# A two-layer hybrid encoder on one core: gate logits turned by full tiles, a projection's first products reordered, and the attention gating moved behind other casts

## The chip, the cores and the metric

The kernel runs on one core of one Trainium2 chip. The core has five engines with queues of their own: TensorE (PE, matrix products; its weight loads are shown apart as PEld), VectorE (DVE), ScalarE (ACT), GpSimd (POOL) and SyncE (SP, which here issues most transfers). The metric is the device time in microseconds of one execution; lower is better. Three runs of the kernel before give a median of 742.87 us.

## The reference

A bidirectional encoder trunk of two layers (`DEPTH = 2`) over 256 tokens and 1024 channels. In each layer the normalised input goes through one wide projection, whose parts feed two branches: a chunked gated DeltaNet that runs over the sequence in both directions, and a differential softmax attention with a partial rotation of q and k. Each branch is normalised and gated by SiLU, projected, weighed by a sigmoid gate and added; one output projection closes the layer.

```python
for l in range(DEPTH):
    h = rmsnorm(x, norm_w[l])
    proj = h @ w_in[l]
    (q_a, k_a, v_a, ab_a, z_a, q_b, k_b, v_b, z_b,
     gate_a, gate_b) = jnp.split(proj, SPLIT_IDX, axis=-1)
    y_a = gated_delta_branch(q_a, k_a, v_a, ab_a, z_a, conv_w[l], a_log[l], dt_bias[l], gdn_norm_w[l])
    lambda_init = 0.8 - 0.6 * math.exp(-0.3 * l)
    y_b = diff_attention_branch(q_b, k_b, v_b, z_b, cos, sin, diff_lambda[l], diff_subln_w[l], lambda_init)
    merged = (jax.nn.sigmoid(gate_a) * (y_a @ w_pa[l])
              + jax.nn.sigmoid(gate_b) * (y_b @ w_pb[l]))
    x = x + merged @ w_out[l]
return rmsnorm(x, final_norm_w)
```

Three places matter here. `ab_a` holds 32 gate logits per token: the rates beta and the decays of 8 heads in two directions. `q_b` is rotated before the attention. The end of the attention branch is

```python
    o = rmsnorm(o, subln_w) * (1.0 - lambda_init)
    o = o.transpose(0, 2, 1, 3).reshape(bsz, seq, DIFF_WIDTH)
    return o * jax.nn.silu(z)
```

## The kernel before

**Products in two halves.** Activations and weights are float32. Each is split into an upper half, the value cast to a shorter form (`hi`), and a lower half, the rest (`lo`), and a product is taken as three: upper by upper (line 324), upper by lower weights (325), lower activations by upper weights (326). A projection of 512 columns (`proj_tm`) goes over eight row blocks of the weights (`kt`) and, in each, over two tiles of 128 tokens (`m`). Its weights come in four pairs of row blocks (`kp`): `weights` loads a pair by a transfer on SP into `raw` (three buffers), casts it on ACT into `hi` (two buffers, line 308) and subtracts on DVE into `lo` (two buffers, line 310). `proj_fm` (385 to 389) does the same with the roles turned, for what the convolutions take.

**What sets the order.** The functions are written as a program, and a scheduler orders each engine's queue when the kernel is built: by priority, which is the order of the text unless a block is marked as of high priority, and by when operands are ready in its own timeline. `behind(x)` orders an instruction behind `x` on the same engine without a wait. On the chip each engine then takes its queue strictly in that order, and a wait stops all that stands behind it. `mark` collects instructions to be named later: `mark[nm, kp]` is the pair (cast on ACT, subtraction on DVE) of the weights of projection `nm`.

**Gate logits.** The 32 columns are projected with both halves of the weights beside each other, so that the sum lies in 64 rows of `abp` (line 630): rows 0 to 31 from the upper half, 32 to 63 from the lower. ACT copies them into `abT` (633), and one fp32 product per token tile with `id2`, two 32x32 identities one above the other, transposes and adds them at once (636). DVE copies the result into `ab` (638).

**The first rotated q.** `qk_part(s_, i)` projects half of q (`s_` = 0) or of k. The first, (0, 0), is written right behind the first half of the convolution's q, while ACT and DVE still evacuate that convolution and ACT takes logarithms and exponentials of the decays (lines 742 and 743). Behind it stand the small fp32 products `kk` of the keys with themselves (787), which have no fixed place.

**Gating the attention.** The attention's output `ob` (two halves `i` of the channels, two token tiles `m`, so four units) is multiplied by the norm's factor `rb` and by the gate `zb` (line 1197, four products on DVE), transposed in 32x32 blocks by DVE (line 249, `send`), written to DRAM on POOL's queue (251) and read back by four transfers on the same queue (257, `fetch`), which completes the transposition. `split_B` then makes its halves: the upper on ACT (263), the lower on DVE (265). All this runs beside the projections of the gates gb and ga, and beside the triangular merges (`join`) and the chunk steps (`chunks`) of the DeltaNet branch, which are of high priority. In that stretch TensorE takes, between the products of gb and ga, the merges y64p, zt, y128p and zt (lines 928, 943, 961), then y1p, sp, ks, y2p, qs and po (992 to 1031). The merges read `T64`, whose blocks DVE transposes at line 954. The sums of the keys' squares (`key_sums`, 1042 to 1054) use the same POOL queue behind the gating.

The places of the four units are given by marks: the gating of unit (0, m) behind the subtraction of pair 2 + m of gb's second half, that of (1, m) behind pair 1 + m of ga's first half; the splits of (0, m) behind pair 2 + m of ga's first half, of (1, m) behind pair 2 + m of its second half.

Of the kernel before, what the change touches and what calls it, by code (L numbers as in the profile page):

```python
# [8 lines left out]
F32 = mybir.dt.float32  # L9
# [3 lines left out]
ALU = mybir.AluOpType  # L13
# [4 lines left out]
P = 128  # L18
DM = 1024
KT = DM // P  # L20
SEQ = 256
NM = SEQ // P
# [27 lines left out]
def hybrid_encoder(  # L50
# [25 lines left out]
    const = pool("const")  # L76
# [18 lines left out]
    def bank_c(name):  # L95
        return ps_c.tile([P, 512], F32, tag="c", name=name)
# [4 lines left out]
    def last(ap, n):  # L101
# [7 lines left out]
    G.memset(ident, 1.0)  # L109
    G.affine_select(out=ident, in_=ident, compare_op=ALU.is_equal, fill=0.0,  # L110
                    base=0, pattern=[[1, P]], channel_multiplier=-1)
    id2 = const.tile([64, 32], F32, name="id2")
    V.tensor_tensor(id2, ident[0:64, 0:32], ident[0:64, 32:64], ALU.add)
    G.memset(tri, 1.0)
    for d, sg in ((0, 1), (1, -1)):
        G.affine_select(out=tri[:, d, :], in_=tri[:, d, :], compare_op=ALU.is_ge,
# [137 lines left out]
    def fetch(tb, dd, after):  # L254
        for j in range(4):
            with behind(after):
                G.dma_start(out=tb[blk(j)], in_=dd[:, :, j].rearrange("i t x -> t i x"))
# [55 lines left out]
                yield 2 * kp + k, hi[:, k, :n], lo[:, k, :n]  # L313

    def proj_tm(act, w, c0, n, evac, nm, places=(None,) * 4, spare=(), later=None, turned=(), between=None,
                banks=None, held=None, first=(), raws={}):

        accs = (banks or banks2)(f"pp_{nm}")
        for kt, hi, lo in weights(w, c0, n, nm, places, later=later, spare=spare, turned=turned, held=held,
                                  first=first, raws=raws):  # L320
            for m in range(NM):
                ts_ = slice(m * P, (m + 1) * P)
                o = accs[m][:, :n]
                T.matmul(o, act[kt // 4][:, 0, kt % 4, ts_], hi, start=kt == 0, stop=False)  # L324
                T.matmul(o, act[kt // 4][:, 0, kt % 4, ts_], lo, start=False, stop=False)  # L325
                mark["proj"] = T.matmul(o, act[kt // 4][:, 1, kt % 4, ts_], hi, start=False,  # L326
                                        stop=kt == KT - 1).ins
                mark["done", nm, kt] = mark["proj"]
        if between:
            between()  # L330
        for m in range(NM):
            evac(m, accs[m][:, :n])
# [174 lines left out]
    for l in range(DEPTH):  # L507
# [86 lines left out]
        def qk_part(s_, i):  # L594
                def evac_qk(m, ps):
                    st = work.tile([P, 512], F32, tag="w2a", name=f"stg{l}{s_}{i}{m}", bufs=2)
                    S.copy(st, ps)
                    g_ = st.rearrange("p (g e) -> p g e", e=DH)
                    x12 = g_[:, :, 0 : 2 * RD].rearrange("p g (x r) -> p g x r", x=2)
                    both = lambda t_: mid(mid(t_[:, m, :], 2), 8)  # L600
                    r4 = small.tile([P, 2, 8, 2, RD], F32, tag="r4", name=f"r4{l}{s_}{i}{m}", bufs=1)
                    V.tensor_tensor(r4[:, 0], x12, both(cos), ALU.mult)
                    V.tensor_tensor(r4[:, 1], x12, both(sin), ALU.mult)
                    V.tensor_tensor(x12[:, :, 0], r4[:, 0, :, 0], r4[:, 1, :, 1], ALU.subtract)
                    V.tensor_tensor(x12[:, :, 1], r4[:, 0, :, 1], r4[:, 1, :, 0], ALU.add)
                    pt = bank(f"qkt{l}{m}{s_}{i}")
                    for b in range(4):
                        T.transpose(pt[:, b * P : (b + 1) * P], st[:, b * P : (b + 1) * P], ident)

                    mark["qkT", m] = S.mul(qkT[i][:, s_, :, m * P : (m + 1) * P],  # L610
                                           pt.rearrange("p (b t) -> p b t", b=4), (DH ** -0.5, 1.0)[s_]).ins
                proj_tm(hT, wl, (C_QB, C_KB)[s_] + 512 * i, 512, evac_qk, f"qk{l}{s_}{i}",
                        turned=(0, 1) if (s_, i) == (0, 1) else ())

# [11 lines left out]
        for kt in range(KT):  # L628
            for part in range(2):
                T.matmul(abp[0:64, :SEQ], wabr[:, kt, :], hT[kt // 4][:, part, kt % 4, :],  # L630
                         start=kt == 0 and part == 0, stop=kt == KT - 1 and part == 1)
        abT = work.tile([64, SEQ], F32, tag="w2c", name=f"abT{l}", bufs=3)
        mark["ab"] = S.copy(abT, abp[0:64, :SEQ]).ins
        abq = bank_c(f"abq{l}")
        for m in range(NM):
            T.matmul(abq[:, m * 32 : (m + 1) * 32], abT[:, m * P : (m + 1) * P], id2,
                     start=True, stop=True)
        V.tensor_copy(ab.rearrange("p m c -> p (m c)"), abq[:, :64])

        a_ = small.tile([P, NM, 32], F32, tag="ga_", name=f"ga_{l}")  # L640
        V.tensor_scalar(a_[:, :, 0:16], ab[:, :, 0:16], -1.0, None, ALU.mult)
# [603 lines left out]
        V.scalar_tensor_tensor(rb, rb, 0.5 * (1.0 - lam0), r0, ALU.mult, ALU.mult)  # L1245

        ybT, yb_sent = pair(f"ybT{l}"), {}
        def gate_yb(i):
            at = [mark[f"ga{l}0", 1 + m][1] if i else mark[f"gb{l}1", 2 + m][1] for m in range(NM)]
            gated(lambda i, m: heads4(ob[i][:, m, :]), zb, rb, nw[:, 1:2], ybT, f"yb{l}",  # L1250
                  after={(i, m): at[m] for m in range(NM)}, halves_=(i,), sent=yb_sent)
            for m in range(NM):
                fetch(*yb_sent[i, m], None)

        gate_yb(0)
        gta = gate(C_GA, f"ga{l}", "eo", (lambda: gate_yb(1), None))
        for i, m in ((0, 0), (0, 1), (1, 0), (1, 1)):
            split_B(ybT[i], yb_sent[i, m][0], m, nw[:, 1:2], mark[f"ga{l}{i}", 2 + m])
        branch(ybT, w_pb[l], gtb, f"pb{l}")
# [137 lines left out]
```

## Time and profile before

| | |
|---|---|
| runs, median (lowest to highest) | 742.87 us (742.01 to 742.99), 3 runs |
| the profiled execution's own time | 742.73 us |
| its span, first to last instruction | 740.8 us |
| mean granted clock of TensorE | 0.997 |
| share of the span, DVE / ACT / POOL | 79% / 65% / 19% |
| transfers | 135.43 MB, mean 183 GB/s |

The page has the busy time of each engine, the span in 40 slices, the transfer queues, the chain of work that ended last, and the costliest groups of instructions. A row of the order of time reads: start in us, duration in us, engine, line, operation, the tile written, the tiles read, their shape, and a count where equal instructions are merged; a bracket gives the engine's idle time before it and what ended it. The ends of matmuls are modelled, so where the time of a matmul matters it is read from the starts of neighbours. A row of the waits reads: engine, tile and line that waited, what it waited for, then the total in us, how often, and the longest.

### The profile page before, as it was taken

The page shows a single profiled execution, that of the slowest core. Times are in us where ns is not written, and L with a number is a line of the kernel's source. Part 1 is how long each engine was busy: PE and PEld are TensorE (multiplying, and loading weights), DVE is VectorE, ACT ScalarE, POOL GpSimd, SP SyncE. Part 2 cuts the span into 40 slices and gives each one's busy share as a digit, 9 for nine tenths or more (in the row PEclk, how much of TensorE's full clock was granted, in tenths as well). Part 3 has the DMA queues.
Part 4 walks back from the last instruction along what each step waited for, and adds up shares of the span by engine and source line. Part 5 has one row for each costly group of instructions (what it writes and reads, how often), then busy time and mean ns, then how long its engine had stood idle before and what let it go on. Part 6 is the DMA issues. An engine that isn't in the chain of part 4 may idle for free.

```text
span 740.8 us, 13649 instructions
## 1 busy us (share of the span) xinstructions
PE 732.1 (99%) x5034; PEld 635.6 (86%) x5034; DVE 588.5 (79%) x1119; ACT 479.5 (65%) x1018; POOL 140.9 (19%) x223
## 2 busy tenths in 40 slices
PE   9999999999999999999999999999999999999996
PEld 6999889987888899888889899889788888998885
DVE  8696898999986885578667769999999769728782
ACT  6666875667876586645456578555787748665552
POOL 6004110112022433100000150202110514311000
PEclk9999999999999999999999999999999999999998
DMA  8755667776766473567674466767766736436641
GB/s 264 239 173 171 172 181 195 209 207 203 208 181 163 136 208 104 173 205 246 201 234 138 129 192 184 212 175 236 200 173 197 203 116 196 150 124 204 213 142 57
DMA packets 73732, 135.43 MB, mean 183 GB/s; under 512 B 12912, under 2 KB 13921, under 8 KB 73666
## 3 DMA queue, kind: packets, MB, share of 16 engines
q1 hardware_dynamic: 64750, 113.65, 51.6%
q0 software_dynamic: 7936, 19.35, 9.1%
q10 hardware_dynamic: 980, 1.58, 0.6%
q8 instruction: 39, 0.64, 0.4%
q14 instruction: 27, 0.22, 0.1%
HBM read 125.53 MB, written 9.01 MB: 182 GB/s over the span
## 4 chain that ended last, share of the span: by engine, by line
PE 96%; ACT 2%; issue 1%; DVE 1%; POOLq 0%; POOL 0%; DVEq 0%; ACTq 0%
PE pp_vb L369 4%; PE pp_qk L325 4%; PE pp_qk L326 3%; PE pp_qk L324 3%; PE sc L1067 2%; PE pp_o L369 2%; PE pp_za L325 2%; PE pf_k L385 2%; PE pf_v L385 2%; PE pf_v L389 2%; PE pp_ga L324 2%; PE pp_gb L324 2%; PE pp_zb L324 2%; PE pf_q L387 2%; PE pf_k L389 2%; PE pf_k L387 2%
## 5 line engine op out<-in xcount | busy, mean ns | idle before, releaser
L325 PE MATMUL pp_qk<-lo_qk,hT 128*128 128x512 f32 x128 | 50.5, 394 | 0.3
L326 PE MATMUL pp_qk<-hi_qk,hT 128*128 128x512 f32 x128 | 49.9, 390 | 0.0
L310 DVE TENSOR_TENSOR lo_qk<-raw_qk,hi_qk 128x1024 fp32r<-128x1024 f32 x32 | 39.1, 1221 | 12.0 <-ACT hi_qk L308 11.7
L324 PE MATMUL pp_qk<-hi_qk,hT 128*128 128x512 f32 x128 | 45.1, 393 | 0.0
L308 ACT CAST hi_qk<-raw_qk 128x1024 fp32r<-128x1024 f32 x28 | 29.4, 1049 | 23.4 <-PE pp_qk L326 12.7
L1077 ACT ACTIVATE es<-sc,mx 128x256 f32<-128x256 f32 x64 | 29.6, 473 | 19.5 <-DVE mx L1075 19.5
L385 PE MATMUL pf_q<-hT,hi_q 128*128 128x256 f32 x128 | 36.1, 285 | 0.0
L387 PE MATMUL pf_q<-hT,hi_q 128*128 128x256 f32 x128 | 35.9, 284 | 0.0
L385 PE MATMUL pf_k<-hT,hi_k 128*128 128x256 f32 x128 | 35.9, 286 | 0.0
L387 PE MATMUL pf_k<-hT,hi_k 128*128 128x256 f32 x128 | 35.9, 285 | 0.0
L385 PE MATMUL pf_v<-hT,hi_v 128*128 128x256 f32 x128 | 35.8, 285 | 0.0
L387 PE MATMUL pf_v<-hT,hi_v 128*128 128x256 f32 x128 | 35.8, 284 | 0.0
L389 PE MATMUL pf_q<-hT,lo_q 128*128 128x256 f32 x128 | 35.2, 288 | 0.0
L310 DVE TENSOR_TENSOR lo_pb<-raw_pb,hi_pb 128x1024 fp32r<-128x1024 f32 x16 | 19.6, 1225 | 18.9 <-ACT hi_pb L308 18.9
L389 PE MATMUL pf_v<-hT,lo_v 128*128 128x256 f32 x128 | 34.6, 288 | 0.0
L389 PE MATMUL pf_k<-hT,lo_k 128*128 128x256 f32 x128 | 34.3, 284 | 0.0
L308 ACT CAST hi_pa<-raw_pa 128x1024 fp32r<-128x1024 f32 x16 | 16.9, 1055 | 22.2 <-PE pp_pa L326 16.1
L679 DVE SCALAR_TENSOR_TENSOR cvq<-pf_q,cw,cvq 128x254 f32<-128x254 f32 (+1 forms) x64 | 30.0, 479 | 0.9 <-ACT cvq L675 0.4
L679 DVE SCALAR_TENSOR_TENSOR cvv<-pf_v,cw,cvv 128x254 f32<-128x254 f32 (+1 forms) x64 | 29.9, 479 | 0.1
L325 PEld LDWEIGHTS pp_qk<-lo_qk,hT 128*128 128x128 f32 x128 | 24.0, 188 | 6.6 <-DVE lo_qk L310 1.6
L679 DVE SCALAR_TENSOR_TENSOR cvk<-pf_k,cw,cvk 128x254 f32<-128x254 f32 (+1 forms) x64 | 28.5, 476 | 1.5 <-ACT cvk L675 0.9
L310 DVE TENSOR_TENSOR lo_pa<-raw_pa,hi_pa 128x1024 fp32r<-128x1024 f32 x16 | 19.6, 1224 | 11.2 <-ACT hi_pa L308 11.2
(416 smaller groups left out, 2535.1 us busy)
## 6 DMA issues: line engine op xcount, KB each, us to landing
raw_qk<-in_w_in_dram SPq DMA_DIRECT2D x32, 512.0 KB, 3.8
raw_k<-in_w_in_dram SPq DMA_DIRECT2D x16, 512.0 KB, 4.6
raw_q<-in_w_in_dram SPq DMA_DIRECT2D x16, 512.0 KB, 3.7
raw_v<-in_w_in_dram SPq DMA_DIRECT2D x16, 512.0 KB, 3.8
raw_zb<-in_w_in_dram SPq DMA_DIRECT2D x16, 512.0 KB, 4.0
raw_za<-in_w_in_dram SPq DMA_DIRECT2D x16, 512.0 KB, 3.8
raw_ga<-in_w_in_dram SPq DMA_DIRECT2D x16, 512.0 KB, 4.6
raw_pb<-in_w_pb_dram SPq DMA_DIRECT2D x16, 512.0 KB, 4.0
```

Source lines behind the costliest of these rows:

```text
L308: high = (V.tensor_copy if kp in turned else S.copy)(hi[:, :, :n], raw[:, :, :n]).ins
L310: mark[nm, kp] = high, V.tensor_tensor(lo[:, :, :n], raw[:, :, :n], hi[:, :, :n].bitcast(F32), ALU.subtract).ins
L324: T.matmul(o, act[kt // 4][:, 0, kt % 4, ts_], hi, start=kt == 0, stop=False)
L325: T.matmul(o, act[kt // 4][:, 0, kt % 4, ts_], lo, start=False, stop=False)
L326: mark["proj"] = T.matmul(o, act[kt // 4][:, 1, kt % 4, ts_], hi, start=False, stop=kt == KT - 1).ins
L369: mark["proj"] = T.matmul(o, act[kt // 4][:, pa, kt % 4, ts_], ws[kt][1 + pw], start=kt == 0 and n_ == 0, stop=kt == KT - 1 and n_ == 2).ins
L385: T.matmul(o, hi[:, cs], act[kt // 4][:, 0, kt % 4, :], start=first, stop=False, skip_group_check=True)
L387: T.matmul(o, hi[:, cs], act[kt // 4][:, 1, kt % 4, :], start=False, stop=False, skip_group_check=True)
L389: T.matmul(o, lo[:, cs], act[kt // 4][:, 0, kt % 4, :], start=False, stop=done, skip_group_check=True)
L679: V.scalar_tensor_tensor(ca[:, o0:o1], acc[:, b, o0 + sft : o1 + sft], cw[:, j, cb : cb + 1], ca[:, o0:o1], ALU.mult, ALU.add)
L1067: mm = T.matmul(sp[n][:, qt * SEQ : (qt + 1) * SEQ], qkT[h // 4][rows, 0, h % 4, qt * P : (qt + 1) * P], qkT[h // 4][rows, 1, h % 4, :], s ...
L1077: S.activation(es[:, n, qt, :], spv[:, qt, :], AF.Exp, bias=mx[:, n, qt : qt + 1], accum_out=s_all[:, h, n, qt : qt + 1])
```

## The change

Three edits.

1. The fold matrix `id2` and the addition that made it go. `abT` becomes a tile of 128 rows whose upper 64 rows POOL sets to zero; each token tile of it is transposed whole by the 128x128 identity, and DVE copies columns 0 to 31 and adds columns 32 to 63.
2. `proj_tm` gets a number `upper`. For the first `upper` row blocks it takes all products with the upper weights (both token tiles, both halves of the activations), and then those with the lower weights. It is 2 for the first half of the rotated q and 0 elsewhere. The same products are summed, in another order.
3. `gate_yb` does one unit at a time, with its reads right behind its write. Unit (0, 0) stays behind pair 2 of gb's second half; the other three follow pairs 0, 1 and 2 of ga's first half, in the order (0, 1), (1, 0), (1, 1), and are written behind the whole of that projection's products. For (1, 0) and (1, 1) these are the marks they had; (0, 1) had pair 3 of gb's second half. The splits keep their marks.

```diff
-    id2 = const.tile([64, 32], F32, name="id2")
-    V.tensor_tensor(id2, ident[0:64, 0:32], ident[0:64, 32:64], ALU.add)
...
     def proj_tm(act, w, c0, n, evac, nm, places=(None,) * 4, spare=(), later=None, turned=(), between=None,
-                banks=None, held=None, first=(), raws={}):
+                banks=None, held=None, first=(), raws={}, upper=0):
 
         accs = (banks or banks2)(f"pp_{nm}")
-        for kt, hi, lo in weights(w, c0, n, nm, places, later=later, spare=spare, turned=turned, held=held,
-                                  first=first, raws=raws):
+        parts = weights(w, c0, n, nm, places, later=later, spare=spare, turned=turned, held=held,
+                        first=first, raws=raws)
+        ws = [next(parts) for _ in range(upper)]
+        for part in range(2 if ws else 0):
+            for kt, hi, lo in ws:
+                for m in range(NM):
+                    for pa in range(2 - part):
+                        mark["proj"] = mark["done", nm, kt] = T.matmul(
+                            accs[m][:, :n], act[kt // 4][:, pa, kt % 4, m * P : (m + 1) * P], lo if part else hi,
+                            start=not (kt or pa or part), stop=False).ins
+        for kt, hi, lo in parts:
             for m in range(NM):
...
-                        turned=(0, 1) if (s_, i) == (0, 1) else ())
+                        turned=(0, 1) if (s_, i) == (0, 1) else (), upper=2 if (s_, i) == (0, 0) else 0)
...
-        abT = work.tile([64, SEQ], F32, tag="w2c", name=f"abT{l}", bufs=3)
-        mark["ab"] = S.copy(abT, abp[0:64, :SEQ]).ins
-        abq = bank_c(f"abq{l}")
+        abT = work.tile([P, SEQ], F32, tag="w2c", name=f"abT{l}", bufs=3)
+        G.memset(abT[64:P], 0.0)
+        mark["ab"] = S.copy(abT[0:64], abp[0:64, :SEQ]).ins
+        abq = bank_c(f"abq{l}")[:, :SEQ].rearrange("p (m c) -> p m c", m=NM)
         for m in range(NM):
-            T.matmul(abq[:, m * 32 : (m + 1) * 32], abT[:, m * P : (m + 1) * P], id2,
-                     start=True, stop=True)
-        V.tensor_copy(ab.rearrange("p m c -> p (m c)"), abq[:, :64])
+            T.transpose(abq[:, m, :], abT[:, m * P : (m + 1) * P], ident)
+        V.tensor_copy(ab, abq[:, :, 0:32])
+        V.tensor_tensor(ab, ab, abq[:, :, 32:64], ALU.add)
...
-        def gate_yb(i):
-            at = [mark[f"ga{l}0", 1 + m][1] if i else mark[f"gb{l}1", 2 + m][1] for m in range(NM)]
+        def gate_yb(i, m, at):
             gated(lambda i, m: heads4(ob[i][:, m, :]), zb, rb, nw[:, 1:2], ybT, f"yb{l}",
-                  after={(i, m): at[m] for m in range(NM)}, halves_=(i,), sent=yb_sent)
-            for m in range(NM):
-                fetch(*yb_sent[i, m], None)
-
-        gate_yb(0)
-        gta = gate(C_GA, f"ga{l}", "eo", (lambda: gate_yb(1), None))
+                  (m,), {(i, m): at}, (i,), yb_sent)
+            fetch(*yb_sent[i, m], None)
+
+        def gate_others():
+            for kp, (i, m) in enumerate(((0, 1), (1, 0), (1, 1))):
+                gate_yb(i, m, mark[f"ga{l}0", kp][1])
+
+        gate_yb(0, 0, mark[f"gb{l}1", 2][1])
+        gta = gate(C_GA, f"ga{l}", "eo", (gate_others, None))
```

## The prediction

> **What bounds the kernel now.** I read the page first, then who waited for whom, then the order of time around each edited place.
>
> ```profile
> span 740.8 us, 13649 instructions
> PE 732.1 (99%) x5034; PEld 635.6 (86%) x5034; DVE 588.5 (79%) x1119; ACT 479.5 (65%) x1018; POOL 140.9 (19%) x223
> PE 96%; ACT 2%; issue 1%; DVE 1%; POOLq 0%; POOL 0%; DVEq 0%; ACTq 0%
> ```
>
> TensorE is busy for 99% of the span and the chain of work that ended last is 96% TensorE. So an edit is worth something only where it shortens TensorE's own row of matmuls or one of the few holes in it. Work that DVE, ACT or POOL gains or loses counts only if TensorE then waits. Among the waits these two rows bear on the change:
>
> ```profile
> PEld pp_qk L325 <- DVE lo_qk L310: 1.6, 4, 0.6
> ACT ybT L263 <- DMA zb<-bny_yb: 2.6, 2, 1.6
> ```
>
> The first is a hole in TensorE's row (four waits for a lower weight half, 1.6 us in all, the longest 0.6). The second is ACT waiting for the attention output's round trip through DRAM, 1.6 us in the first layer and 1.0 in the second. It costs TensorE nothing by itself, but it says that this round trip is already late where ACT wants it.
>
> **Part 1, gate logits by full tiles.** Order of time on PE; the first columns are start and duration in us.
>
> ```profile
> 27.17 0.28 PE L389 MATMUL pf_k<-hT,lo_k 128*128 128x256 f32 x1
> 27.38 0.63 PE L636 MATMUL abq<-id,abT 64*128 64x32 f32 x4
> 27.94 0.39 PE L385 MATMUL pf_k<-hT,hi_k 128*128 128x256 f32 x1
> 28.16 0.28 PE L387 MATMUL pf_k<-hT,hi_k 128*128 128x256 f32 x1
> 28.28 0.28 PE L389 MATMUL pf_k<-hT,lo_k 128*128 128x256 f32 x1
> ...
> 69.55 0.28 PE L389 MATMUL pf_q<-hT,lo_q 128*128 128x256 f32 x1
> 69.67 0.38 PE L706 MATMUL ctk<-ident,kq 128*128 128x128 f32 x2
> 69.81 0.36 PE L385 MATMUL pf_q<-hT,hi_q 128*128 128x256 f32 x1
> 70.01 0.28 PE L387 MATMUL pf_q<-hT,hi_q 128*128 128x256 f32 x1
> ```
>
> Matmuls overlap, so I go by starts. A 256-column product follows its predecessor by 0.12 us (28.16 to 28.28). From the product at 27.17 to the second one behind the logits, 28.16, pass 0.99 us, of which two ordinary steps are 0.24: the two fp32 products with the folding matrix cost 0.75 us (four records, two passes each). The change puts two full 128x128 transposes by the identity there, and these the trace has in the same surroundings: 69.55 to 70.01 is 0.46, less 0.24 is 0.22 us. The gain is 0.53 us a layer, **1.06 us** for two. The bounds are 0 (if the two transposes end up where TensorE would have waited anyway) and 1.06.
>
> ```profile
> L902 POOL MEMSET T<- 32x256 f32 x4 | 1.3, 317 | 0.1
> 28.05 0.22 DVE L638 COPY ab<-abq 128x64 f32<-128x64 f32 x1
> ```
>
> What it adds elsewhere: a memset of 64x256 on POOL (a 256-element one took 317 ns), and on DVE an addition beside the copy, some 0.2 us each. POOL is 19% busy and the memset depends on nothing but its slot, so it is hidden; if it came late the transposes would wait behind it, up to its 0.3 us a layer. The fold that left the kernel's opening was 64x32 on DVE and stood ahead of nothing that TensorE waits for there; 0. The Trainium skill's page "TensorE: Matmul & The Clock Gate", section "Part 4: PE-mode transpose", gives a 128x128 transpose some 275 ns in a kernel's context. By that, as an estimate, two would cost 0.55 us and the part would give 0.4 us in all instead of 1.06. The row above has the pair at 0.22, overlapped, and the sum goes by the row.
>
> **Part 2, products with upper weights first.** DVE, PE and ACT rows at the first rotated q of layer 0, then the twin of the wait in layer 1.
>
> ```profile
> 72.31 1.23 DVE L310 TENSOR_TENSOR lo_qk<-raw_qk,hi_qk 128x1024 fp32r<-128x1024 f32 x1 [2.59 <-ACT hi_qk L308]
> ...
> 73.84 0.63 PE L324 MATMUL pp_qk<-hi_qk,hT 128*128 128x512 f32 x2
> ...
> 78.61 1.04 ACT L308 CAST hi_qk<-raw_qk 128x1024 fp32r<-128x1024 f32 x1
> ...
> 79.68 1.22 DVE L310 TENSOR_TENSOR lo_qk<-raw_qk,hi_qk 128x1024 fp32r<-128x1024 f32 x1
> ...
> 80.20 0.61 PE L324 MATMUL pp_qk<-hi_qk,hT 128*128 128x512 f32 x2
> 80.96 0.50 PE L325 MATMUL pp_qk<-lo_qk,hT 128*128 128x512 f32 x1
> 81.29 0.39 PE L326 MATMUL pp_qk<-hi_qk,hT 128*128 128x512 f32 x1
> 81.52 0.40 PE L325 MATMUL pp_qk<-lo_qk,hT 128*128 128x512 f32 x1
> ```
> ```profile
> 443.25 0.19 PEld L325 LDWEIGHTS pp_qk<-lo_qk,hT 128*128 128x128 f32 x1 [0.56 <-DVE lo_qk L310]
> ```
>
> The edit reorders the first two row blocks only. Their lower half was ready at 73.54, before the stage's first product (73.84), so there is no wait to remove at that place, and the count of products is the same. The hole is at the fifth row block: two products from 80.20 should be followed 0.46 later (0.23 each, 81.29 to 81.52), at 80.66; the next starts at 80.96, and the step behind it is 0.33 instead of 0.23. That is 0.40 us a layer. The reorder reaches it indirectly: the upper half's buffer (two of them) is last read by the eighth product instead of the twelfth, some 0.9 us earlier, so the cast for the third pair (78.61, behind table loads and convolution work on ACT) may be placed earlier; and the small fp32 products that now fill the first pair's order may move into the hole. The cast needs to come only 0.3 us earlier. Bounds: 0 (order on ACT unchanged) to 0.40 a layer; below nothing by a disturbed convolution, which I take as small since DVE has the same work. I take the upper end, **0.8 us** for both, as the hole is so short.
>
> **Part 3, the gating.** Four units, each 4 products and a 32x32 transposition on DVE, a write to DRAM and four reads on POOL's queue, then a split on ACT and DVE. Unit (0,1) moves from behind the last lower half of the second gb projection to behind the first of ga; the other three keep their marks, but the reads of (0,0) no longer stand behind the write of (0,1).
>
> ```profile
> 248.90 1.99 DVE L249 STREAM_TRANSPOSE zb<-ob 128x512 f32<-128x512 f32 x2
> 250.92 0.43 DVE L954 STREAM_TRANSPOSE T<-U__96 32x256 f32<-32x256 f32 x1
> ```
> ```profile
> 252.22 1.79 PE L961 MATMUL y128p<-T,A 64*64 64x64 f32 x64
> 253.95 0.50 PE L324 MATMUL pp_ga<-hi_ga,hT 128*128 128x512 f32 x1
> ...
> 258.95 1.17 PE L961 MATMUL zt<-U__96,y 64*64 64x64 f32 x64
> 260.05 0.50 PE L324 MATMUL pp_ga<-hi_ga,hT 128*128 128x512 f32 x1
> ```
>
> Today the two units stand ahead of the four transpositions of T on DVE (the first at 250.92), and the merge y128p needs these. Its 64 products take 1.73 us to the next start (252.22 to 253.95), while the 64 of zt, same form, take 1.10 (258.95 to 260.05). So up to 0.63 us a layer is waiting. With one unit gone the transpositions start up to 2 us earlier. Bounds 0 and 0.63; what is late next is ga's first lower half on DVE, which today follows those transpositions, so I take two thirds, 0.4 a layer, **0.8 us**.
>
> The sum: 742.73 us is the profiled execution's own time (its span is 740.8); less 1.06, 0.8 and 0.8 is 740.1. The median of the runs shown, 742.87, is 0.14 above that execution, so the forecast is **740.2 us**.
>
> **The rivals.** *The round trip comes too late (slower).* The unit (0,1) now queues on DVE behind ga's first lower half, and then behind the scalings of ktm and the second lower half, which are of high priority. It would then be sent about where (1,0) is today.
>
> ```profile
> 260.08 0.56 POOL L251 DMA_DIRECT2D bny_yb<-zb  x1 [2.73 <-DMA wb_n<-in_norm_w_dram]
> 265.41 2.17 POOL L257 DMA_DIRECT2D zb<-bny_yb  x4 [4.77 <-DMA bny_yb<-zb]
> ```
> ```profile
> zb<-bny_yb POOLq DMA_DIRECT2D x2, 64.0 KB, 4.2
> ```
> ```profile
> 264.35 1.27 ACT L263 ACTIVATE ybT<-zb,nw 128x512 fp32r<-128x512 f32 x1
> 265.50 1.05 ACT L308 CAST hi_ga<-raw_ga 128x1024 fp32r<-128x1024 f32 x1
> 266.44 0.59 ACT L1000 COPY A<-y1p 128x512 f32<-128x512 f32 x1
> ```
> ```profile
> 268.53 1.05 PE L992 MATMUL sp<-A,ktm 128*128 128x128 f32 x8
> ...
> 270.80 2.84 PE L992 MATMUL sp<-A,ktm 128*128 128x128 f32 x24
> ```
>
> Sent at 260.08, read from 265.41 on, the last read issued near 267.0 and landing 4.2 later: 271.2. ACT's split of (0,1) stands at 264.35, with the next cast and the four copies of y1p behind it, and the products sp wait for those. The first copy ends at 267.03, needed at 268.53: ACT may be 1.5 us late, and from there TensorE pays. If the split keeps its place it is 6.9 late: 5.4 a layer, 751.0 in the end. If it lands behind the first copy, the second copy ends at 271.2 + 1.27 + 0.59 = 273.1 against 270.80: 2.3 a layer, 4.6 in all, **744.8 us** (740.2 + 4.6). Behind the third copy it costs nothing. For it speaks that ACT waited for this trip in both layers already and that the split's mark is unchanged; against it that ACT's order is worked out anew at build time, and that (0,0) now comes home earlier, which frees up to 1.6 us on ACT.
>
> The page "DMA: Bandwidth & Descriptors", section "Anatomy of one DMA — SWDGE (gpsimd) path" of the Trainium skill, gives such a transfer about 2.0 us plus its bytes at 436 GB/s. By that, as an estimate, the write takes 2.6 and a read 2.15, the unit is home near 266.9, and this rival shrinks to about 1 us a layer in its worst place; the trace's write took 4.8 and its read 4.2, beside weight loads.
>
> *The holes stay (same).* The hole of part 2 needs another order on ACT and that of part 3 an earlier first lower half of ga; if neither comes, only the transposes are left: 742.87 - 1.06 = **741.8 us**, and a small new wait on ACT brings it nearer to 743. That the change does not do what it says is part of this: upper products first where no lower half is late.
>
> **How the numbers follow.** About 0.2%, 1.5 us, is what a measurement of this kernel can tell from no change. The forecast has 0.45, the late round trip 0.28, the staying holes 0.27. Faster by over 0.2% is the forecast, 0.45; slower is the late trip, 0.28; the rest 0.27. Without loss the bounds of the three parts reach down to 742.87 - 1.06 - 0.80 - 1.26 = 739.75, and I start the range just below, at 739.5; upward it goes past 744.8 into the worse placements, to 746.5, leaving out some 0.15 for the worst. The forecast's own range is 739.5 to 741.4.
>
> **What would show it.** Right: two records in place of four at the logits and some 0.46 us between their neighbours two steps apart; no wait of pp_qk on lo_qk near 80; y128p's 64 products in about 1.1 to 1.3 us; no long wait of ACT for the second unit. Wrong: ACT waiting 2 us or more on the reads of zb with sp starting late behind it, or reads of the key sums (which queue on POOL behind the units) holding DVE ahead of the ks products. A new order of POOL or ACT elsewhere in the layer, which no row of before can show, would also upset it.

## The result, and the profile after

The changed kernel takes 744.49 us (median of 9 runs, 743.99 to 746.18), the kernel before beside it 742.74 (742.01 to 743.92, 9 runs): a ratio of 1.0023, with a 95% interval of 1.0014 to 1.0032. It is slower by 1.75 us; the forecast was 740.2 and faster.

From the page of the changed kernel, whose span is 742.0 us: TensorE's and the other engines' busy time, and the chain of work that ended last, by engine.

```profile
PE 731.1 (99%) x5030; PEld 634.6 (86%) x5030; DVE 587.8 (79%) x1120; ACT 479.2 (65%) x1018; POOL 140.7 (19%) x225
...
PE 87%; DVE 5%; ACT 3%; issue 2%; POOL 1%; DMA 1%; SPq 0%; POOLq 0%; DVEq 0%; ACTq 0%
```

TensorE is busy for 1.0 us less than before and the span is 1.2 us longer, so TensorE waits more. The chain says the same: it was 96% TensorE and is 87%, with 5% on DVE. The waits say where.

```profile
PEld pp_qk L332 <- DVE lo_qk L308: 2.7, 4, 1.1
PEld pp_ga L332 <- DVE lo_ga L308: 2.2, 2, 1.1
...
ACT ybT L261 <- DMA zb<-bny_yb: 0.6, 1, 0.6
```

The wait of the rotated q for a lower half grew from 1.6 us to 2.7 (the longest from 0.6 to 1.1). A wait of ga for a lower half is new: two, one a layer. The wait of ACT for the round trip through DRAM, the prediction's slow rival, shrank from 2.6 to 0.6. Stage by stage, layer 0:

**Part 1 came as forecast.** Order of time on PE at the gate logits; lines 392 to 396 are those that were 385 to 389.

```profile
26.68 0.28 PE L396 MATMUL pf_k<-hT,lo_k 128*128 128x256 f32 x1
26.80 0.38 PE L644 MATMUL abq<-ident,abT 128*128 128x128 f32 x2
...
27.14 0.28 PE L394 MATMUL pf_k<-hT,hi_k 128*128 128x256 f32 x1
```

26.68 to 27.14 is 0.46 us where it was 0.99: 0.53 won, in each layer. The Trainium skill's page "TensorE: Matmul & The Clock Gate" (section "Part 4: PE-mode transpose") has some 275 ns for each. By that, as an estimate, the pair would have cost 0.55; it adds 0.22 to the row here.

**Part 2 moved the hole and made it longer.** Order of time on PE, then on ACT, then on DVE, at the first rotated q. (Line 324 has the products of the new order, 331 to 333 are the old 324 to 326; 306 is the cast, 308 the subtraction, 683 to 698 the convolution.)

```profile
72.82 2.00 PE L324 MATMUL pp_qk<-hi_qk,hT 128*128 128x512 f32 x8
...
79.19 0.62 PE L331 MATMUL pp_qk<-hi_qk,hT 128*128 128x512 f32 x2
79.64 0.39 PE L332 MATMUL pp_qk<-lo_qk,hT 128*128 128x512 f32 x1
...
81.91 0.61 PE L331 MATMUL pp_qk<-hi_qk,hT 128*128 128x512 f32 x2
83.21 0.50 PE L332 MATMUL pp_qk<-lo_qk,hT 128*128 128x512 f32 x1 [0.68 <-DVE lo_qk L308]
83.54 0.39 PE L333 MATMUL pp_qk<-hi_qk,hT 128*128 128x512 f32 x1
```
```profile
76.92 1.04 ACT L306 CAST hi_qk<-raw_qk 128x1024 fp32r<-128x1024 f32 x1
77.86 0.41 ACT L693 ACTIVATE thq<-cvq 128x256 f32<-128x256 f32 x1
...
79.58 0.47 ACT L683 ACTIVATE cvq<-pf_q,cw 128x256 f32<-128x256 f32 x1 [0.85 <-DVE kq L698]
79.96 1.04 ACT L306 CAST hi_qk<-raw_qk 128x1024 fp32r<-128x1024 f32 x1
```
```profile
79.47 2.56 DVE L687 SCALAR_TENSOR_TENSOR cvq<-pf_q,cw,cvq 128x254 f32<-128x254 f32 x6
81.94 1.22 DVE L308 TENSOR_TENSOR lo_qk<-raw_qk,hi_qk 128x1024 fp32r<-128x1024 f32 x1
```

The fifth row block has no hole any more: the product with its lower half follows 0.45 us behind the pair of 79.19. But at the seventh, the pair at 81.91 should be followed at 82.36 and is at 83.21: 0.85 late, and the step behind it is 0.33 for 0.23. That is 0.95 a layer in place of 0.40. ACT shows why. The third cast now stands ahead of the convolution's tanh (line 693), where it stood behind it and behind the next block's first product. So `kq` comes later (79.13, which is 6.3 us behind the stage's first product; before, 78.38, it was 4.5). ACT waits 0.85 us for it before it can begin the third block, and the fourth cast stands behind that; on DVE the fourth subtraction stands behind six convolution products in a row. Before, four stood there:

```profile
80.82 1.64 DVE L679 SCALAR_TENSOR_TENSOR cvq<-pf_q,cw,cvq 128x255 f32<-128x255 f32 x4
82.38 1.21 DVE L310 TENSOR_TENSOR lo_qk<-raw_qk,hi_qk 128x1024 fp32r<-128x1024 f32 x1
```

Counted from the stage's first product, the fourth subtraction starts at 82.38 - 73.84 = 8.54 us before and at 81.94 - 72.82 = 9.12 after.

**Part 3 made ga's third lower half late.** PE, then DVE.

```profile
251.85 1.48 PE L969 MATMUL y128p<-T,A 64*64 64x64 f32 x64
253.26 0.50 PE L331 MATMUL pp_ga<-hi_ga,hT 128*128 128x512 f32 x1
...
256.70 1.44 PE L969 MATMUL zt<-U__94,y 64*64 64x64 f32 x64
258.07 0.50 PE L332 MATMUL pp_ga<-lo_ga,hT 128*128 128x512 f32 x1
...
260.49 0.61 PE L331 MATMUL pp_ga<-hi_ga,hT 128*128 128x512 f32 x2
261.77 0.50 PE L332 MATMUL pp_ga<-lo_ga,hT 128*128 128x512 f32 x1 [0.67 <-DVE lo_ga L308]
262.11 0.39 PE L333 MATMUL pp_ga<-hi_ga,hT 128*128 128x512 f32 x1
```
```profile
257.60 1.14 DVE L1205 SCALAR_TENSOR_TENSOR ob<-ob,rb,zb 128x128 f32<-128x128 f32 x4
258.65 2.02 DVE L247 STREAM_TRANSPOSE zb<-ob 128x512 f32<-128x512 f32 x2
260.51 1.21 DVE L308 TENSOR_TENSOR lo_ga<-raw_ga,hi_ga 128x1024 fp32r<-128x1024 f32 x1
```

y128p is shorter, 1.41 us to the next start (1.73 before). But ahead of ga's third lower half DVE now has the transpositions of two units in place of one, and it starts at 260.51 where it started at 259.61, while TensorE is there 0.36 earlier. The pair at 260.49 should be followed at 260.94 and is at 261.77: 0.83 late, and the step behind it is 0.34 for 0.23, 0.94 in all. zt takes 1.37 us (256.70 to 258.07) where it took 1.10. Together 0.94 + 0.27 - 0.32 = 0.89 a layer lost, 1.8 in all.

### The profile page after: what moved, and what is told of

Its sections match the earlier page's. It is cut to its first block, busy times and chain, and to the rows that moved or that the text cites. A ratio compares the mean times of both kernels' runs of the same rounds, so it can differ in the third digit from the quotient of the medians.

```text
span 742.0 us, 13645 instructions
## 1 busy us (share of the span) xinstructions
PE 731.1 (99%) x5030; PEld 634.6 (86%) x5030; DVE 587.8 (79%) x1120; ACT 479.2 (65%) x1018; POOL 140.7 (19%) x225
## 4 chain that ended last, share of the span: by engine, by line
PE 87%; DVE 5%; ACT 3%; issue 2%; POOL 1%; DMA 1%; SPq 0%; POOLq 0%; DVEq 0%; ACTq 0%
PE pp_vb L376 4%; PE pp_qk L332 3%; PE pp_qk L333 3%; PE pp_qk L331 3%; PE sc L1075 2%; PE pp_o L376 2%; PE pf_v L392 2%; PE pp_za L332 2%; PE pf_k L392 2%; PE pf_v L396 2%; PE pp_zb L331 2%; PE pf_k L396 2%; PE pf_q L394 2%; PE pf_k L394 2%; PE pf_v L394 2%
## 5 line engine op out<-in xcount | busy, mean ns | idle before, releaser
L332 PE MATMUL pp_qk<-lo_qk,hT 128*128 128x512 f32 x120 | 47.2, 393 | 1.4 <-DVE lo_qk L308 1.4
L333 PE MATMUL pp_qk<-hi_qk,hT 128*128 128x512 f32 x120 | 46.8, 390 | 0.0
L331 PE MATMUL pp_qk<-hi_qk,hT 128*128 128x512 f32 x120 | 42.2, 393 | 0.0
L332 PEld LDWEIGHTS pp_qk<-lo_qk,hT 128*128 128x128 f32 x120 | 22.5, 188 | 7.4 <-DVE lo_qk L308 2.7
```

## The experiments

Each kernel was run several times beside the kernel before on the same chip (one was run once, where that is said); its ratio is to those runs, with its 95% interval, and can differ by up to 0.0006 from the quotient of the two medians. The median of before was 742.64 to 742.91 in all of them.

### One part at a time

The edits are the three parts of the change's diff, alone; and the change without `upper`.

> Only the gate logits by full transposes (and the fold matrix gone from the opening). Theory: the losses belong to the other two parts, so this part keeps its 0.53 us a layer, 1.06 in all, and perhaps the 0.4 us by which the opening of the changed kernel was earlier: ratio 0.9980 to 0.9986, some 741.3 to 741.7 us. Rival (whatever TensorE gains is waited for again at the next late lower half, since ACT and DVE are not earlier): ratio 0.9995 to 1.0005.

Measured: 741.44 us, ratio 0.9985 (0.9976 to 0.9993). The theory holds; the gain is not waited for again.

> Only upper weights first at the first two row blocks of the first rotated q. Theory: the hole moves from the fifth to the seventh row block and grows, because DVE's last lower half of this stage stands behind six convolution products; 0.58 us a layer lost, ratio 1.0012 to 1.0018, some 743.9 us, and a wait of pp_qk on lo_qk near 83. Rival (the loss needs part 1, which brings TensorE to this place 1 us earlier than before): no loss, ratio 0.9985 to 1.0003, no wait above 0.4 us.

Measured: 743.81 us, 1.0015 (1.0006 to 1.0023). The theory holds, also in its place. PE in this kernel, where the wait stands without part 1:

```profile
83.93 0.50 PE L334 MATMUL pp_qk<-lo_qk,hT 128*128 128x512 f32 x1 [0.68 <-DVE lo_qk L310]
```

> Only the moved gating unit. Theory: y128p is 0.3 us a layer shorter, but the third lower half of the first ga projection now stands on DVE behind two units of the gating in place of one: a wait of pp_ga on lo_ga of 0.8 us a layer and a later merge, 1.25 us a layer lost, net 0.95 a layer: ratio 1.0020 to 1.0028, some 744.6 us. First rival (the late round trip of the prediction): ACT waits 2 us or more for the reads of zb and the products sp start late; 744.8 or more, with no wait on lo_ga. Second rival (the loss needs part 1): ratio 0.9985 to 1.0000.

Measured: 744.41 us, 1.0026 (1.0016 to 1.0035). From this kernel's waits:

```profile
ACT ybT L263 <- DMA zb<-bny_yb: 2.3, 2, 1.7
PEld pp_ga L325 <- DVE lo_ga L310: 2.2, 2, 1.1
```

The new wait is there, and ACT's waits for the round trip are in sum no longer than before (2.3 for 2.6 us; the longest 1.7 for 1.6), so the first rival falls here, and the second by the time.

> Part 2 undone alone. Theory (the parts add up): what part 2 lost, 0.6 us a layer, comes back: 744.5 - 1.2 = 743.3 us, ratio 1.0003 to 1.0012, with the wait on lo_ga as in the changed kernel and the hole of the rotated q at the fifth row block again. Rival (the stages do not add up, an earlier arrival at the gating only lengthens the wait there): ratio above 1.0015.

Measured: 743.50 us, 1.0013 (1.0004 to 1.0022), at the upper end of what the theory gives. The parts add up: -1.22 + 1.15 + 1.75, each against its own runs of before, is +1.68; the change has +1.75.

### Part 2: is it the order of the products, or the earlier cast?

`later` names, by pair, the instruction on ACT behind which that pair's cast has to stand. Here the third pair's cast (2) is held behind the first product of the convolution's second block.

```diff
-                    S.activation(ca, acc[:, b, :], AF.Copy, scale=cw[:, 2, cb : cb + 1])
+                    mark["tap", seg, g, j4] = S.activation(ca, acc[:, b, :], AF.Copy, scale=cw[:, 2, cb : cb + 1]).ins
...
-                        turned=..., upper=2 if (s_, i) == (0, 0) else 0)
+                        turned=..., upper=2 if (s_, i) == (0, 0) else 0,
+                        later={2: (mark["tap", "q", 0, 1], None)} if (s_, i) == (0, 0) else None)
```

> Parts 1 and 2, with ACT's cast of the third pair held behind the first product of the second convolution block, which is where it stands before the change; nothing else. Theory (part 2 lost by the earlier cast, which pushed the convolution back on ACT and DVE, and not by the order of the products): the 0.4 us hole comes back at the fifth row block, the longer one at the seventh goes, and the time is that of part 1 alone, 741.4 us, ratio 0.9980 to 0.9988. Rival (the order of the products or the moved kk costs by itself): 742.5 us or more, ratio above 0.9994.

Measured: 741.45 us, 0.9985 (0.9976 to 0.9993), the time of part 1 alone. PE in this kernel, at the fifth row block and at the seventh:

```profile
79.74 0.61 PE L331 MATMUL pp_qk<-hi_qk,hT 128*128 128x512 f32 x2
80.49 0.50 PE L332 MATMUL pp_qk<-lo_qk,hT 128*128 128x512 f32 x1
...
82.89 0.62 PE L331 MATMUL pp_qk<-hi_qk,hT 128*128 128x512 f32 x2
83.35 0.40 PE L332 MATMUL pp_qk<-lo_qk,hT 128*128 128x512 f32 x1
```

The old hole is back (0.75 us for 0.45) and the long one is gone (0.46). In this kernel ACT, DVE, POOL and SP take the same instructions in the same order as in part 1 alone, and only TensorE's products stand in another; so the products' order by itself costs and gains nothing that can be measured. The fourth subtraction starts 8.56 us after the stage's first product here (73.36 to 81.92), 8.54 in part 1 alone, and 9.12 in part 2 alone as in the change.

The same with the mark of the third block, `mark["tap", "q", 0, 2]` (run once; the name of the run is not that of its edit):

> Parts 1 and 2, with ACT's cast of the third pair held one convolution block further back, behind the first product of the third block. Theory: the third lower half is then the late one, the hole at the fifth row block is longer than the 0.4 us of before, and the time is above part 1 alone by that much: 742 to 744 us. Rival (the place of this cast does not matter): 741.4 us.

Measured: 743.07 us in one run, with a wait of 1.01 us at the fifth row block. So in these three kernels the place of this one cast sets which lower half is late.

Next, upper weights first where a lower half is late. `upper` becomes a set of pairs, each taken as the change takes the first: eight products with the upper weights, then four with the lower.

```diff
-        ws = [next(parts) for _ in range(upper)]
-        for part in range(2 if ws else 0):
...
+        for kt, hi, lo in parts:
+            if kt // 2 in upper:
+                ws = [(kt, hi, lo), next(parts)]
+                for part in range(2):
...
-                        ..., upper=2 if (s_, i) == (0, 0) else 0)
+                        ..., upper=(2,) if (s_, i) == (0, 0) else ())
```

> Part 1, and upper weights first at the third pair of row blocks (the fifth and sixth) of the first rotated q, where the hole is, in place of the first pair. Theory: there the lower half is needed eight products (1.8 us) after the pair begins and is ready 0.4 us late in the kernel before, so the wait of pp_qk on lo_qk near 80 goes and no other lower half is late: 741.44 - 0.8 = 740.6 us, ratio 0.9970 to 0.9977. Rival (as with the first pair, the hole only moves on to the seventh row block): ratio 0.9984 to 0.9995 and a wait near 83.

Measured: 741.38 us, 0.9984 (0.9975 to 0.9992): not to be told from part 1 alone. The rival holds. PE in this kernel:

```profile
82.40 0.61 PE L334 MATMUL pp_qk<-hi_qk,hT 128*128 128x512 f32 x2
83.06 0.38 PE L395 MATMUL pf_q<-hT,hi_q 128*128 128x256 f32 x1
...
83.40 0.40 PE L335 MATMUL pp_qk<-lo_qk,hT 128*128 128x512 f32 x1
```

The fourth pair's lower half is now the late one, and two products of the next projection (83.06 and 83.28) stand in the hole.

> Part 1, and upper weights first at the third and the fourth pair of the first rotated q. Theory: the lower halves of both pairs are then needed 1.8 us after their pair begins, so neither is late and the 0.3 to 0.4 us a layer of the hole is won: 740.6 to 740.8 us, ratio 0.9970 to 0.9980. Rival (DVE's supply is late for the stage as a whole, so that the next projection's lower halves wait instead): ratio 0.9983 to 0.9990.

Measured: 740.99 us, 0.9977 (0.9969 to 0.9986). As the theory says, but the interval overlaps that of part 1 alone, and below this piece adds nothing to others; it stays open whether it is a gain.

### Part 3: the late lower half, and the round trip

Upper weights first at the third pair of ga's first half (`upper=(2,)` there); DVE's order is the same as in parts 1 and 3.

> Parts 1 and 3, and upper weights first at the third pair of row blocks of the first ga projection, whose lower half comes late behind two units of the gating; the order on DVE is the same as in parts 1 and 3 alone. Theory: the wait of 0.83 us a layer on lo_ga goes, 743.50 - 1.66 = 741.8 us, ratio 0.9984 to 0.9994. Rival (this wait only hides a later one, the copies of y1p or the round trip): ratio above 1.0005.

Measured: 741.14 us, 0.9984 (0.9975 to 0.9992). The wait is gone and 2.36 us of 743.50 with it, more than the wait and its slower step (1.9). Where the other 0.5 comes from is not shown.

Then the other repair: the two units behind the moved one go one pair later.

```diff
         def gate_others():
             for kp, (i, m) in enumerate(((0, 1), (1, 0), (1, 1))):
-                gate_yb(i, m, mark[f"ga{l}0", kp][1])
+                gate_yb(i, m, mark[f"ga{l}0", kp + (kp > 0)][1])
```

> Parts 1 and 3, with the two units behind the moved one each one pair of row blocks later, so that DVE has four products and one transposition ahead of ga's third lower half, as before the change. Theory: the wait on lo_ga and the longer merge zt go, 1.1 us a layer, and y128p keeps its 0.3: 740.8 to 741.4 us, ratio 0.9974 to 0.9984. Rival (the late round trip): ACT's split of unit (0,1) stands ahead of the copies of y1p in this order and waits for the reads of zb, sp is late by 1 us a layer or more: ratio above 0.9995.

Measured: 745.69 us, 1.0044 (1.0032 to 1.0057). The wait on ga's lower half is gone, and the rival came in its place. ACT and PE in this kernel:

```profile
269.20 1.20 ACT L261 ACTIVATE ybT<-zb,nw 128x512 fp32r<-128x512 f32 x1 [4.48 <-DMA zb<-bny_yb]
...
270.83 1.05 ACT L999 COPY A<-y1p 128x512 f32<-128x512 f32 x2
```
```profile
271.44 4.33 PE L991 MATMUL sp<-A,ktm 128*128 128x128 f32 x32 [1.28 <-ACT A L999]
```

The scheduler has put the split of unit (0,1) ahead of the copies of y1p, ACT stands 4.48 us for the reads, and sp waits for the copies. With both repairs in one kernel (this one and upper weights first at the third pair of the rotated q):

> All three with both repairs: part 1, upper weights first at the third pair of the first rotated q, and the moved unit with the two behind it one pair later. Theory (the stages add up): 741.44 - 0.8 - 0.3 to 0.6: 740.0 to 740.4 us, ratio 0.9963 to 0.9970. Rival (the moved unit costs through the round trip): not faster than part 1 with the third pair alone.

Measured: 745.27 us, 1.0031 (1.0019 to 1.0043), with ACT waiting up to 5.1 us. The rival holds, by the same cause. Now the split alone is moved:

```diff
-            split_B(ybT[i], yb_sent[i, m][0], m, nw[:, 1:2], mark[f"ga{l}{i}", 2 + m])
+            split_B(ybT[i], yb_sent[i, m][0], m, nw[:, 1:2], mark[f"ga{l}1", 1] if (i, m) == (0, 1) else mark[f"ga{l}{i}", 2 + m])
```

> The spread units again (parts 1 and 3, the two units behind the moved one each one pair later), with ACT's and DVE's split of unit (0,1) held behind the second lower half of the second ga projection, that is behind the four copies of y1p. Theory (the round trip costs by the place of the split on ACT alone): ACT's 4.5 us wait and the late sp go, 745.7 - 4.4 = 741.3 us, ratio 0.9974 to 0.9986. Rival (the units one pair later are late at the output projection too): ratio above 0.9995.

Measured: 741.37 us, 0.9982 (0.9973 to 0.9990). The theory holds: 4.3 us for the place of one split a layer, which is an instruction on ACT and one on DVE. (The scheduler then moved some other instructions too, products of ks and y2p among them; what these are worth is not shown.) This is the prediction's rival, which the change itself escaped: on ACT in the changed kernel that split stands behind the second copy and has no wait.

```profile
269.11 1.22 ACT L261 ACTIVATE ybT<-zb,nw 128x512 fp32r<-128x512 f32 x1
```

### Everything together

The change with the third cast held and upper weights first at ga's third pair:

> The changed kernel with all three parts, and both causes found taken out: the third cast of the rotated q held where it stood before, and upper weights first at the third pair of the first ga projection. Theory (these two account for the whole loss): 744.49 - 1.2 x 2 halves of part 2's loss (2.36 in all with ga's 2.36 = 4.4 at most, 3.3 by the runs of the parts alone): 741.1 to 741.4 us, ratio 0.9976 to 0.9986. Rival (something else of the change still costs, or the two interact): ratio above 0.9992.

Measured: 741.47 us, 0.9980 (0.9972 to 0.9989). The two causes account for the whole loss. But no more than part 1's gain is left:

> Part 1, part 3, and upper weights first where a lower half is late and nowhere else: third and fourth pair of the first rotated q, third pair of the first ga projection. Theory (the gains add up): 741.14 - 0.45 = 740.7 us, ratio 0.9968 to 0.9980, below every other version. Rival (part 3 with its wait repaired gives nothing over part 1): 741.0 us, ratio 0.9975 to 0.9985, not separable from part 1 with the third and fourth pair.

Measured: 741.41 us, 0.9985 (0.9976 to 0.9994). The rival holds: part 3 with its wait repaired gives nothing over part 1 that can be measured. PE in part 1 alone, and then in parts 1 and 3 with upper weights first at ga:

```profile
251.47 1.76 PE L960 MATMUL y128p<-T,A 64*64 64x64 f32 x64
253.16 0.50 PE L322 MATMUL pp_ga<-hi_ga,hT 128*128 128x512 f32 x1
...
258.17 1.17 PE L960 MATMUL zt<-U__94,y 64*64 64x64 f32 x64
259.27 0.50 PE L322 MATMUL pp_ga<-hi_ga,hT 128*128 128x512 f32 x1
```
```profile
251.47 1.48 PE L972 MATMUL y128p<-T,A 64*64 64x64 f32 x64
252.87 0.50 PE L334 MATMUL pp_ga<-hi_ga,hT 128*128 128x512 f32 x1
...
256.31 1.44 PE L972 MATMUL zt<-U__94,y 64*64 64x64 f32 x64
257.69 0.50 PE L335 MATMUL pp_ga<-lo_ga,hT 128*128 128x512 f32 x1
```

y128p wins 0.29 (1.69 to 1.40), zt gives 0.28 back (1.10 to 1.38). Each has 32 products (the 64 records) in two groups, `g`. In the instruction streams zt of the faster kind begins with 3, 2, 1, 2, 2, 2 of the groups in turns; the slower zt, and y128p in the kernels above, run 8 of one, 8 of the other, and only then in turns. So the order was written out:

```diff
             def quarters(ps, lhs, rhs, row):
-                for c, j4, g, d in every4:
-                    with behind(mark["pin"]):
-                        T.matmul(ps[g][...], lhs(g, d, c, j4), rhs(g, d, c, j4), start=True, stop=True)
+                last = mark["pin"]
+                for c, j4, g, d in sorted(every4, key=lambda e: (e[0], e[1], -e[2], -e[3])):
+                    with behind(last):
+                        last = T.matmul(ps[g][...], lhs(g, d, c, j4), rhs(g, d, c, j4),
+                                        start=True, stop=True).ins
```

> Parts 1 and 3 with upper weights first at the third pair of the first ga projection, and the 64x64 products of y128p and zt in an order written out: two of the one group, two of the other, in turns, zt beginning with the group that is evacuated last. Theory (these 64 products take 1.10 us where the groups alternate, as zt before the change, and 1.37 to 1.41 where eight of one group stand together): y128p 1.40 to 1.10 and zt 1.38 to 1.10, 0.58 us a layer: 741.14 - 1.16 = 740.0 us, ratio 0.9958 to 0.9970, a step of 1.1 us from the first of y128p to the next ga product. Rival (the 1.4 is set by the waits for T and y and not by the order): no change, ratio 0.9980 to 0.9988.

Measured: 744.31 us, 1.0017 (1.0009 to 1.0026). PE in this kernel, at zt (y128p goes from 251.54 to 252.64):

```profile
258.72 1.16 PE L973 MATMUL zt<-U__94,y 64*64 64x64 f32 x64
259.81 2.11 PE L326 MATMUL pp_ga<-hi_ga,hT 128*128 128x512 f32 x8
```

The theory of the length holds: both take 1.10 and 1.09 us. The time does not follow, since zt, bound to begin with the group that is evacuated last, was placed ten ga products later (258.72 for 256.31), and what needs it came later too. The profiled execution was the fastest of this kernel (742.78 us; the runs go up to 745.51), so what the slower ones add is not shown.

> Part 1 with the same order of y128p and zt, and the gating as before the change. Theory: zt alternates there already, and y128p waits for the last transposition of T, which ends about 0.5 us behind its first product; with the groups in turns that wait comes at the second pair, and 0 to 0.2 us a layer are won: 741.0 to 741.4 us, ratio 0.9977 to 0.9986. Rival (order alone sets y128p): 0.5 us a layer, ratio 0.9970 to 0.9975.

Measured: 744.25 us, 1.0017 (1.0006 to 1.0027), with runs from 742.65 to 746.64. Neither theory. zt came later here too (259.33 for 258.17), but the longest wait of TensorE there is due to the round trip again. ACT now has the split of unit (0,1) ahead of the evacuation of zt, where it stood behind it, and waits 3.56 us for the reads; y1p waits for that evacuation, 2.8 us in both layers together. ACT, then PE:

```profile
264.11 1.21 ACT L261 ACTIVATE ybT<-zb,nw 128x512 fp32r<-128x512 f32 x1 [3.56 <-DMA zb<-bny_yb]
```
```profile
265.85 1.16 PE L992 MATMUL y1p<-vtm,U__94 128*128 128x128 f32 x8 [1.96 <-ACT U__94 L978]
```

Last, y128p's groups in turns and zt as it was; no other instruction of any engine changes its place.

> As parts1and3_upper_ga, with the two groups of y128p's products in turns, and nothing else: every other instruction of every engine stands where it stood (zt keeps its place and its order). Theory: y128p takes 1.10 instead of 1.40 us, nothing is moved behind it, and 0.3 us a layer come through: 741.14 - 0.6 = 740.5 us, ratio 0.9966 to 0.9978. Rival (the next wait, for y or ga's lower halves, takes it): ratio 0.9980 to 0.9988.

Measured: 741.58 us, 0.9984 (0.9975 to 0.9992). The rival holds. PE in this kernel:

```profile
251.64 1.16 PE L973 MATMUL y128p<-T,A 64*64 64x64 f32 x64
252.74 0.50 PE L334 MATMUL pp_ga<-hi_ga,hT 128*128 128x512 f32 x1
```

y128p is 0.30 us shorter, and y1p starts at 262.67, 0.15 us earlier than without this, though y128p began 0.17 later in this execution. But at the end of sp the 0.3 us are gone again: sp reads what ACT copies from y1p, and ACT begins the first of these copies 15.8 us behind the start of y128p in both kernels.

> The same with upper weights first at the third and fourth pair of the first rotated q too. Theory (the pieces add up): 740.0 to 740.5 us, ratio 0.9962 to 0.9975. Rival (as best_of_the_pieces: the rotated q adds nothing that a measurement can tell): within 0.3 us of the other run.

Measured: 741.46 us, 0.9982 (0.9973 to 0.9990). The rival again. All ten versions that came out faster than the kernel before lie between 740.99 and 741.58 us. They beat it by 1.1 to 1.7 us; part 1 alone has 1.2, and what they have beyond it can't be told from nothing.

## Why the prediction was wrong, point by point

The sum had three gains, 1.06, 0.8 and 0.8 us. The first came (1.22); the second came as a loss of 1.15 and the third as one of 1.75.

- **Part 1** was right in size and place: 1.06 forecast from a step of 0.46 us between neighbours, 0.46 found, 1.22 us in the run of it alone. The memset and the added DVE addition cost nothing that shows.
- **Part 2**: the step that failed is "below nothing by a disturbed convolution, which I take as small since DVE has the same work". The mechanism of the gain came as put (the third cast is placed earlier, the hole at the fifth row block closes). But DVE's same work in another order starts the fourth lower half 0.58 us later, and that one had only 0.22 us of slack: before, it ended at 82.38 + 1.21 = 83.59 and was needed at 83.81. TensorE, with the first hole closed, also comes 0.43 us sooner. So 0.8 us of gain became 1.15 of loss. That the earlier cast does it, and not the products' order, is shown by holding the cast. The sign that was named for this part, no wait near 80, came true while the part lost.
- **Part 3**: two steps failed. "What is late next is ga's first lower half on DVE": it is the third, behind two units in place of one, with 0.94 us a layer. I had it in the rival that the unit "queues on DVE behind ga's first lower half" and did not ask what then stands behind the unit. It had little slack: before, it ended at 259.61 + 1.23 = 260.84, and its first product was at 261.08. And the term "up to 0.63 us a layer is waiting" was mis-sized: it compared y128p with zt, "same form", but of another order; the wait was 0.32 (1.73 to 1.41), and the other 0.3 is the order of the two groups, as the last runs show. Even the 0.32 did not last: the scheduler placed zt earlier and in the slower order, and zt took 0.27 longer.
- **The round trip** was the wrong reason for "slower". The unit was sent where the prediction had it (POOL issues the write at 260.04, forecast 260.08), and the mechanism is real: in the kernel with the spread units a split ahead of all copies costs 4.3 us in two layers. The size was not: for that place the prediction had 5.4 a layer, and its 4.6 in all was for a place "behind the first copy". (There the unit was written at 259.25 and read from 262.91 on, 3.7 us later, where the prediction had counted with 5.3.) In the changed kernel ACT's order was worked out anew, as the prediction had it against this rival, and the split has no wait. That 744.49 lies inside the range and near this rival's 744.8 is luck, since another cause made it.
- **Holes stay** (741.8) is where the change comes out with the two new waits removed: 741.47. The gains that the sum had for parts 2 and 3 came clearly in no version.

## What to carry to other kernels

When an edit brings one supply forward, list the next supplies of the same engine with their slack, ended against needed: here the next lower half had 0.22 us, and the one after the moved gating 0.24, while the edits made them start 0.6 and 0.9 us later. In this kernel the hole in TensorE's row marked the rate of the engines that feed it: closing it moved the wait to the next pair, in the change as well as with upper weights first at the third pair. And a bound taken from "the same form elsewhere" needs the same order of instructions, not only the same shapes and count.

## What the runs showed of the hardware that I had not expected

The 64 records of 64x64 fp32 products take 1.10 us when the two groups, each of which uses two other quarters of the array, come in turns by two, and 1.37 to 1.41 when eight products of one group stand together; changing y128p's order alone changes its length from 1.40 to 1.10 (251.64 to 252.74 in that kernel). The Trainium skill's page "TensorEngine Tiling (Array Packing)", section "Tiling Modes", says that different tiles of the array can load weights and multiply in parallel; the runs agree, and add that here the gain depended on the order of the queue: it was there in full only where neighbours went over all four tiles.

The first products of pp_vb, in the opening, start at 8.76 us in the profile of before and at 8.33 in that of the changed kernel. Over all twenty profiled executions they start between 8.27 and 9.42 us, and kernels with the same opening differ as much among themselves. So these 0.43 us can't be put down to the change, and the spans of two single profiles can't show a difference below about 1 us.

The 256 KB write of a unit took about 2.7 us from its issue to the issue of the reads behind it (248.96 to 251.62 on POOL in the changed kernel), where the row that the prediction quoted has 5.3 (260.08 to 265.41). The Trainium skill's page "DMA: Bandwidth & Descriptors" (section "Anatomy of one DMA — SWDGE (gpsimd) path") makes that 2.6, as an estimate, and this write agrees. The one that the prediction quoted took 4.8 us from issue to landing alone; why it was slower is not shown by a run here.
